# Row-wise infinity norm of an 8192 x 8192 matrix: other runs of rows, another list of tail loads, eight load semaphores for five

## The chip, the core and the metric

One Trainium2 chip, one NeuronCore of it. The engines that matter here are VectorE (DVE in the profile), which reduces; GpSimd (POOL), which combines partial results; SyncE (SP) and ScalarE (ACT), whose queues issue DMAs; and the core's 16 DMA engines, which move data between DRAM and SBUF. SBUF has 128 partitions; a tile is written "partitions x columns". The metric is the device time of one execution in microseconds (us), as a median of several; lower is better.

## The reference

```python
def setup_inputs():
    return {"x": np.random.randn(8192, 8192).astype(np.float32)}

def reference(x):
    return np.linalg.norm(x, ord=np.inf, axis=1)
```

With `axis=1` the infinity norm of a row is the largest absolute value in it. So 268 MB of float32 are read, each element once, and 8192 numbers come out.

## The kernel before

**Which row lies where.** The kernel splits the rows into a main part and a tail of `ROWS` x 128 rows. In both, a partition holds consecutive rows of `x`, which lie in DRAM without a gap: 46 rows a partition in the main part, 18 in the tail. A row is 8192 columns, 32 KiB. Neighbouring partitions therefore read from addresses that lie 46 x 32 KiB and 18 x 32 KiB apart.

**Main part.** 23 loads of two rows a partition (16384 columns, 64 KiB a partition, 8.4 MB in all) go to `ring`, a buffer in SBUF of `RING` = 3 x 16384 columns, so to three places in turn. Each is reduced by one `tensor_reduce` (maximum of absolute values), which writes two numbers a partition to `res_big`.

**Tail.** The 18 rows of a partition are taken as one line of 147,456 columns and cut into loads of falling size. `tail_loads` plans the cuts: from the last load (`FIRST` = 768 columns) backwards, it makes each load as large as the reductions behind it leave time for, by the prices `LOAD` and `REDUCE` (us a column, us fixed). The result is 29 loads, in the order of issue of 16384, 10048, 14528, 8192 (3 times), 8448, 9088, 8064, 7168, 5632, 5696, 5056, 4224, 3968, 3136 (twice), 2752, 2496, 2176, 1920, 1600, 1472, 1344, 1152, 1024, 896, 768 and 704 columns. The load before the last is the end of the last row but one; the last load is the end of the last row.

A load can hold the end of a row, whole rows, and the beginning of another; `parts` lists these pieces, each with its own reduction. Where a row has several pieces, their results go to a small tile `parts<row>`, and GpSimd combines them with `tensor_scalar` (L207), up to two more values in one instruction. The last row differs: the results of its earlier pieces are written in `ring` just behind the place of the last load (`spots`, beyond `RING`), so that the last reduction takes the 704 loaded columns and the 6 results beside them at once, 710 elements.

**Order and waits.** `Pieces.load` issues each load on SP's queue and has it add 16 to one of `SEMS` = 5 semaphores, used in turn. `Pieces.reduce` waits on that semaphore. A load waits for two things: that the reduction of the load five before it is done (one load at a time on a semaphore, L97 to L103), and that the columns of the ring which it overwrites have been reduced (the framework finds that). `Pieces.room` gives places in the ring one after another; where the rest is too short for a load, it starts at 0 again. All loads are in one queue: SP issues them in order, so a load that waits holds up those behind it.

**The end.** ACT stores `res_big` and the first `ROWS` - 2 columns of `res_tail`, both after the reduction of the load two before the last (L221, L225, L229). SP waits for GpSimd's last combination (L236) and for VectorE, stores the last two columns (L240), and waits for ACT's stores and its own.

Of the kernel before, what the change touches and what calls it, by code (L numbers as in the profile page):

```python
# [8 lines left out]
R = 2  # L9
RING = 3 * 16384  # L10
APART = 2048
SEMS = 5


LOAD = (1.1775e-3, 0.073)
REDUCE = (1.0417e-3, 0.060)
SPARE = 0.08
ROWS = 18
FIRST = 768
SNAP = 0.6  # L20
GRAIN = 64

IDLE = 2


def tail_loads(n_cols, big):

    slack = 0.0
    lag = REDUCE[0] * FIRST + REDUCE[1]
    loads = []
    end = ROWS * n_cols

    def take(top, bottom, most):
        nonlocal slack  # L40
        w = 0
        n = 0
        spare = SPARE if loads else 0
        while True:

            n += 1
            start = max(bottom, (top - 1) // n_cols * n_cols - (n - 1) * n_cols)
            fit = int((lag + slack - spare - REDUCE[1] * n) / REDUCE[0])
            w = max(w, min(fit, top - start) // GRAIN * GRAIN)
            if fit <= top - start or start <= bottom:  # L50
                break
        w = max(GRAIN, min(w, most, top - bottom))
        row = (top - w + n_cols - 1) // n_cols * n_cols
        if top - row >= SNAP * w or (w == most and top > row):
            w = top - row
        n = (top - 1) // n_cols - (top - w) // n_cols + 1
        slack += (LOAD[0] - REDUCE[0]) * w + LOAD[1] - REDUCE[1] * n
        loads.append((top - w, w))
        return top - w

    ends = [take(end, end - n_cols, FIRST), take(end - n_cols, end - 2 * n_cols, n_cols)]
    for top, bottom in zip(ends, (end - n_cols, 0)):
        while top > bottom:
            top = take(top, bottom, big)
    return loads[::-1]


class Pieces:
# [7 lines left out]
    def __init__(self, tc, ring):  # L76
        self.tc, self.nc, self.ring, self.head = tc, tc.nc, ring, 0
        self.sems = [tc.alloc_semaphore(f"loaded{i}") for i in range(SEMS)]
        self.started = self.reduced = 0
# [9 lines left out]
    def load(self, at, w, src):  # L89
        i = self.started  # L90
        self.started += 1
        ins = self.nc.sync.dma_start(out=self.ring[:, at : at + w], in_=src)  # L92
        ins.then_inc(self.sems[i % SEMS], 16)
        self.tc.no_tile_sem_insts.add(ins.ins.name)
        self.tc.declare_no_dep(ins.ins, group="loads", reason="a reduction stands in between")
        self.tc.add_to_no_dep_group("loads", ins.ins)
        if i >= SEMS:  # L97
            self.tc.add_manual_dep(
                ins.ins,
                self.last[i - SEMS].name,  # L100
                mybir.DependencyInfo(mybir.DependencyClass.Sync, mybir.DependencyReason.DATA),
# [3 lines left out]
    def reduce(self, pairs):  # L105
# [3 lines left out]
        for k, (dst, src) in enumerate(pairs):  # L109
# [9 lines left out]
            else:  # L119
                ins.wait_op(self.sems[i % SEMS], 16 * (i // SEMS + 1), "sem-ge")  # L120
            self.tc.declare_no_dep(ins.ins, group="loads", reason="waits on the load's semaphore")
# [5 lines left out]
def kernel(  # L127
# [6 lines left out]
    f32 = mybir.dt.float32  # L134
    n_rows, n_cols = x.shape

    tail = tail_loads(n_cols, R * n_cols)
    split = n_rows - ROWS * P
    n_big = split // (R * P)

# [7 lines left out]
    res_big = single.tile([P, n_big, R], f32)  # L148
    res_tail = single.tile([P, ROWS], f32)
    idle = single.tile([1, IDLE], f32)  # L150
    pieces = Pieces(tc, ring)

    for t in range(n_big):
        at = pieces.room(R * n_cols)
# [6 lines left out]
    for i, (start, w) in enumerate(tail):  # L161
        c = 0
        while c < w:
            row = (start + c) // n_cols
            n = min(w - c, (row + 1) * n_cols - start - c)
            parts.append((row, i, c, n))
            c += n
    of_row = [[q for q in parts if q[0] == row] for row in range(ROWS)]

# [3 lines left out]
    at = RING  # L173
    for row, own in enumerate(of_row):
        if row == ROWS - 1:
            spots[own[-1][1]] = at
# [13 lines left out]
    for i, (start, w) in enumerate(tail):  # L190
        at = spots[i] if i in spots else pieces.room(w)
# [7 lines left out]
        )  # L199
        for row in range(ROWS - 1):  # L200
            if len(of_row[row]) > 1 and of_row[row][-1][1] == i:
# [78 lines left out]
```

## Time and profile before

| | us |
|---|---|
| median of 3 runs (628.87 to 628.91) | 628.88 |
| the profiled execution | 628.88 |
| its span on the chip | 627.1 |
| DVE busy | 552.1 (62 instructions) |
| POOL busy | 3.2 (14 instructions) |
| DVE waiting for loads before the 23 big reductions | 69.4 (22.5 of it for the first) |
| DVE waiting for loads in the tail | 2.1 and 1.2 |

The page gives, for each engine, busy time and its share of the span; for 40 equal slices the busy share in tenths; and for each group of instructions the source line, engine, operation, `output<-input` by tile name, shape and count, then busy time, mean ns of one, and the idle time before them with what ended it. `L110` is line 110 of the kernel. A `q` behind an engine's name (`SPq`) means its queue, which issues DMAs. The busy time by stretch has, in this order: the stretch in us from the span's start, its length, DVE's busy time (and instructions), POOL's, the clock granted to the matrix engine (not used here), the DMA engines' busy share and the GB/s that they moved. The order of time has: start, duration, engine, line, operation, tiles, shape and count, and in brackets the idle time before.

The waits on SP's own queue show what holds loads back: 455.9 us for reductions of `res_big`, 82.3 for those that write `parts`, 59.2 for those that write `res_tail`, 3.8 for those that write `ring`; the longest single one is 37.7 us. The loads' time from issue to landing is 21.8 us for the first, about 40.8 for big ones, and 4.1 for the last.

### The profile page before, as it was taken

The numbers are of one execution on the slowest core, as the hardware profiler recorded it, in microseconds if no ns is written. First come the engines' busy times: TensorE is split into PE (matmuls) and PEld (weight loads), VectorE is DVE, ScalarE is ACT, GpSimd is POOL, SyncE is SP. The second block draws the span as 40 slices with busy tenths as digits, with TensorE's granted clock in tenths as the row PEclk, the third lists the DMA queues.
The fourth block names the chain that finished last, engine by engine and source line by source line (L and its number), as shares of the span: only waits on it lengthen the run. The fifth ranks groups of instructions, "written<-read, shape, count | busy, mean of one in ns | idle before, by whom it ended". The sixth has DMA issues, their size and how long they took to land.

```text
span 627.1 us, 175 instructions
## 1 busy us (share of the span) xinstructions
DVE 552.1 (88%) x62; POOL 3.2 (1%) x14
## 2 busy tenths in 40 slices
DVE  0588988889988889888898888988889999999998
POOL 0000000000000000000000000000000000000000
DMA  9999999999999999999999999999999999999997
GB/s 401 410 460 401 468 401 468 401 468 401 468 401 468 401 468 401 468 401 468 401 464 405 451 418 451 418 439 431 422 437 442 404 435 442 430 422 430 426 422 308
DMA packets 7921, 268.48 MB, mean 428 GB/s; under 512 B 1264, under 2 KB 1264, under 8 KB 2416
## 3 DMA queue, kind: packets, MB, share of 16 engines
q1 hardware_dynamic: 7632, 268.44, 99.3%
q10 hardware_dynamic: 288, 0.03, 0.0%
q14 instruction: 1, 0.01, 0.0%
HBM read 268.44 MB, written 0.03 MB: 428 GB/s over the span
## 4 chain that ended last, share of the span: by engine, by line
DMA 57%; DVE 42%; issue 0%; DVEq 0%; SPq 0%
DMA ring<-in_x_dram 57%; DVE res_big L110 22%; DVE parts L110 12%; DVE res_tail L110 7%; DVE ring L110 1%; DVEq L275 0%; SPq L92 0%; DVE idle L218 0%
## 5 line engine op out<-in xcount | busy, mean ns | idle before, releaser
L110 DVE TENSOR_REDUCE res_big<-ring 128x2 f32<-128x16384 f32 x23 | 396.1, 17220 | 69.4 <-DMA ring<-in_x_dram 69.4
L110 DVE TENSOR_REDUCE parts<-ring 128x1 f32<-128x3136 f32 (+18 forms) x22 | 78.5, 3634 | 1.2 <-DMA ring<-in_x_dram 1.2
L110 DVE TENSOR_REDUCE res_tail<-ring 128x1 f32<-128x8192 f32 (+1 forms) x9 | 69.8, 7811 | 2.1 <-DMA ring<-in_x_dram 2.1
L110 DVE TENSOR_REDUCE ring<-ring 128x1 f32<-128x1600 f32 (+5 forms) x6 | 8.3, 1445 | 0.0
L207 POOL TENSOR_SCALAR res_tail<-parts 128x1 f32<-128x1 f32 x9 | 2.7, 296 | 615.6 <-DVE parts L110 615.6
L207 POOL TENSOR_SCALAR parts<-parts 128x1 f32<-128x1 f32 x1 | 0.4, 353 | 5.6 <-DVE parts L110 5.6
L264 POOL MEMSET const-bfloat16-1.0<- 128x1 bf16 x1 | 0.1, 101 | 0.0
L264 POOL MEMSET const-uint8-127<- 128x1 uint8 x1 | 0.1, 101 | 0.0
L264 POOL MEMSET const-float32-0.0<- 128x1 f32 x1 | 0.1, 99 | 0.2 <-issue 0.2
L264 POOL MEMSET const-float32-1.0<- 128x1 f32 x1 | 0.1, 98 | 0.0
L218 DVE MEMSET idle<- 1x1 f32 x2 | 0.1, 59 | 0.0
## 6 DMA issues: line engine op xcount, KB each, us to landing
ring<-in_x_dram SPq DMA_DIRECT2D x3, 4096.0 KB, 40.5
ring<-in_x_dram SPq DMA_DIRECT2D x1, 7264.0 KB, 31.1
ring<-in_x_dram SPq DMA_DIRECT2D x1, 5024.0 KB, 33.3
ring<-in_x_dram SPq DMA_DIRECT2D x1, 4544.0 KB, 34.6
ring<-in_x_dram SPq DMA_DIRECT2D x1, 4224.0 KB, 40.3
ring<-in_x_dram SPq DMA_DIRECT2D x1, 4032.0 KB, 35.5
ring<-in_x_dram SPq DMA_DIRECT2D x1, 3584.0 KB, 35.4
ring<-in_x_dram SPq DMA_DIRECT2D x2, 1568.0 KB, 18.3
```

The lines of the kernel that those rows point to most:

```text
L110: ins = self.nc.vector.tensor_reduce(out=dst, in_=src, axis=mybir.AxisListType.X, op=mybir.AluOpType.max, apply_absolute_value=True,)
L207: combined = nc.gpsimd.tensor_scalar(out=to, in0=best, scalar1=two[0], scalar2=two[1] if len(two) == 2 else None, op0=mybir.AluOpType.max, ...
L218: rest = nc.vector.memset(idle[:, i : i + 1], 0.0)
L264: nc = _bacc.Bacc("TRN2", target_bir_lowering=False, num_devices=1)
```

## The change

The tail has 16 rows a partition instead of 18, so the main part has 48 instead of 46 and 24 big loads instead of 23. `tail_loads` no longer plans: a written list `TAIL` of 28 sizes takes its place, from 13504 columns to two of 640. The function lays them one after another; the load before the last is the last 640 columns of the last row but one, as before in kind, and the last row is begun before it. `SEMS` is 8. Nothing else is changed; the code that makes pieces, places, waits and stores works from these values. By it, VectorE has 66 reductions instead of 60 and GpSimd 14 combinations instead of 10; the last reduction takes 640 loaded columns and 7 results.

```diff
-SEMS = 5
-
-
-LOAD = (1.1775e-3, 0.073)
-REDUCE = (1.0417e-3, 0.060)
-SPARE = 0.08
-ROWS = 18
-FIRST = 768
-SNAP = 0.6
-GRAIN = 64
+SEMS = 8
+
+
+ROWS = 16
+TAIL = [13504, 13632, 12160, 10816, 9664, 8576, 7616, 6784, 6080, 5376, 4800, 4288, 3776, 3392]
+TAIL += [2944, 2624, 2368, 2048, 1792, 1152, 1472, 1280, 1088, 960, 832, 768, 640, 640]
...
-def tail_loads(n_cols, big):
...
+def tail_loads(n_cols):
+    last_row = (ROWS - 1) * n_cols
+    loads = []
+    at = 0
+    for w in TAIL[:-2]:
+        loads.append((at, w))
+        at += w
+        if at + TAIL[-2] == last_row:
+            at = last_row
+    loads += [(last_row - TAIL[-2], TAIL[-2]), (at, TAIL[-1])]
+    assert sum(TAIL) == at + TAIL[-1] == ROWS * n_cols
+    return loads
...
-    tail = tail_loads(n_cols, R * n_cols)
+    tail = tail_loads(n_cols)
```

More of the change, by code (lines that the diff above doesn't have):

```diff
@@ L11 @@
 APART = 2048
-SEMS = 5
-LOAD = (1.1775e-3, 0.073)
-REDUCE = (1.0417e-3, 0.060)
-SPARE = 0.08
-ROWS = 18
-FIRST = 768
-SNAP = 0.6
-GRAIN = 64
+SEMS = 8
+ROWS = 16
+TAIL = [13504, 13632, 12160, 10816, 9664, 8576, 7616, 6784, 6080, 5376, 4800, 4288, 3776, 3392]
+TAIL += [2944, 2624, 2368, 2048, 1792, 1152, 1472, 1280, 1088, 960, 832, 768, 640, 640]
 IDLE = 2
-def tail_loads(n_cols, big):
-    slack = 0.0
-    lag = REDUCE[0] * FIRST + REDUCE[1]
+def tail_loads(n_cols):
+    last_row = (ROWS - 1) * n_cols
     loads = []
[L37 to L65, printed above, removed]
+    at = 0
[7 more added lines that the diff above has]
+    return loads
 class Pieces:
```

## The prediction

> **What bounds the kernel now.** I read the page's head and the row of slices first, then the busy time by stretch, then the instructions in order of time, then the rows by shape. The page says that one thing never stops:
>
> ```profile
> span 627.1 us, 175 instructions
> DVE 552.1 (88%) x62; POOL 3.2 (1%) x14
> DMA  9999999999999999999999999999999999999997
> HBM read 268.44 MB, written 0.03 MB: 428 GB/s over the span
> ```
>
> The DMA engines are full in every slice but the last, VectorE works 88% of the span. The busy times of three stretches (big loads; the first two tail loads; the rest) show what changes on the way:
>
> ```profile
> 22.50:467.60 445.10, 396.05 (x23) 0.00 (x0) 1.00 1.00 433
> 467.60:496.70 29.10, 27.88 (x5) 0.00 (x0) 1.00 0.99 428
> 496.70:624.90 128.20, 128.20 (x35) 3.02 (x10) 1.00 0.99 422
> ```
>
> The reader is to see that DMA keeps its pace (433 GB/s, 422 with small loads), while VectorE, idle 49 us of the first 445, is busy for all of the last 128.2. Both end together, and the order of time shows how closely:
>
> ```profile
> 22.50 17.22 DVE L110 TENSOR_REDUCE res_big<-ring 128x2 f32<-128x16384 f32 x1 [22.50 <-DMA ring<-in_x_dram]
> 41.85 17.22 DVE L110 TENSOR_REDUCE res_big<-ring 128x2 f32<-128x16384 f32 x1 [2.13 <-DMA ring<-in_x_dram]
> ...
> 467.62 25.87 DVE L110 TENSOR_REDUCE res_tail<-ring 128x1 f32<-128x8192 f32 x3 [2.13 <-DMA ring<-in_x_dram]
> 493.41 2.08 DVE L110 TENSOR_REDUCE parts<-ring 128x1 f32<-128x1856 f32 x1
> 496.68 6.75 DVE L110 TENSOR_REDUCE parts<-ring 128x1 f32<-128x6336 f32 x1 [1.20 <-DMA ring<-in_x_dram]
> ...
> 623.27 0.37 ACTq L221 DMA_DIRECT2D out_dram<-res_big  x1
> ...
> 624.01 0.89 DVE L110 TENSOR_REDUCE res_tail<-ring 128x1 f32<-128x710 f32 x1
> ...
> 624.84 0.06 DVE L218 MEMSET idle<- 1x1 f32 x2
> 624.92 0.35 SPq L240 DMA_DIRECT2D out_dram<-res_tail  x1
> ```
>
> Big loads arrive every (467.62 - 22.50)/23 = 19.353 us and are reduced in 17.22. From 496.68 VectorE never waits visibly. The trace's landing records show that the loads do not run far ahead: the last one lands at 623.95, 0.06 before its reduction. So the end is the last landing, plus 0.06, plus one reduction of 0.89, plus what follows it (627.10 - 624.90 = 2.20), plus 628.88 - 627.10 = 1.78 outside the span. The profiled execution took 628.88, the median of the runs.
>
> **Prices.** Loads: from one landing to the next, 16384 columns take 19.354 us and 768 take 0.98, a line of about 0.073 us + 1.1775 ns a column; it meets the 28 landings between to about 0.02 us; the last load, with none behind it, is 0.06 cheaper. Reductions:
>
> ```profile
> L110 DVE TENSOR_REDUCE parts<-ring 128x1 f32<-128x7936 f32 x1 | 8.4, 8409 | 0.0
> L110 DVE TENSOR_REDUCE parts<-ring 128x1 f32<-128x768 f32 x1 | 0.9, 945 | 0.0
> L110 DVE TENSOR_REDUCE res_tail<-ring 128x1 f32<-128x710 f32 x1 | 0.9, 885 | 0.0
> ```
>
> (8409 - 945)/(7936 - 768) = 1.041 ns a column and 0.145 us fixed. Neighbours overlap: three of 8192 fill 467.62 to 493.41, 8.597 each, so one costs 0.06 us + 1.0417 ns a column of VectorE's time, and the last one of a row of them 0.085 more.
>
> **The change part by part.**
>
> *Number and bytes of loads: nothing.* Before, 23 + 29 = 52 loads; after, 24 + 28 = 52, of the same 524,288 columns. At the line above all landings add up to the same, and the last stays at 623.95 if the queue never runs dry and a column costs what it did.
>
> *Does VectorE keep up with the new list?* I walked both lists with these prices (landing after landing; a reduction starts 0.02 after its landing or when the one before lets it). The walk gives the old kernel's last landing as 623.95 and its end as 624.90, as measured. For the new list: the 13504 columns land at 483.6, VectorE comes free from the last big one at 484.9; the 13632 land at 499.72 when it has been idle 0.7; from there 117,568 columns in 40 reductions need 117,568 x 1.0417 ns + 40 x 0.06 + 0.085 = 124.96 us, so they could end at 499.75 + 124.96 = 624.71. The other path is the last landing, 623.95 + 0.03 + the last reduction. So VectorE's six extra instructions (66 reductions for 60, 0.36 us) lie in idle time before 499.75 and in some 0.09 us after. Without that cover they would cost 0.36.
>
> *A shorter last load.* 640 columns and 7 partial results are 647 instead of 710: 63 x 1.0417 ns = 0.066 us less.
>
> *Start after landing.* 0.06 before, 0.03 in the walk. Along the new list the walk's lag is 0.02 to 0.09 (0.58 once, at 1152), so this is between 0.04 gained and 0.03 lost; I take -0.03, the place's own value.
>
> *The ring.* The 10816 columns no longer fit behind 12160 (50,112 of 49,152), go to place 0, and leave 9,856 columns unused, so that load must wait for the 13504 to be reduced, to 499.2. On SP the seven loads behind it wait as well. It is needed once the load before it has landed at 514.1, less 2.4 us of start (21.78 us from the first issue to the first reduction, less 19.35): 511.7, so 12.5 us cover the wait; without them it would cost its lateness one for one.
>
> *Eight semaphores.* They let a load be issued three reductions earlier. The walk finds the closest issue 4.4 us ahead of need (0.8 before, with none late), and with five it ends at the same time: no gain. What seven loads in flight instead of four cost isn't shown: from below nothing (the pace was one line with two, three or four in flight), from above a second 0.073 for each of 28, 2.0 us. I take nothing, the nearer row.
>
> *Stores.* ACT's two wait for the reduction of the load two before the last, now of 768 columns; it ends at 623.33 by the walk, some 0.15 later than before. The first store took until 1.6 us after issue, the second 2.1; so the second is done near 626.0, before SP's last at 624.8 + 1.4 = 626.2. Were they 0.3 later, they would decide. GpSimd makes 14 combinations for 10, the last of 0.36 us from 624.24 to 624.60, 0.19 before VectorE ends.
>
> *Where the rows lie.* A partition's rows in DRAM start 48 x 32 KiB = 1536 KiB apart instead of 1472, and in the tail 512 KiB instead of 576. No row has these distances. From below, nothing: 1472 and 576 agree (the first tail load, 16384 columns, lands 19.36 us after its forerunner; a 64 KiB packet takes 2.42 us in both, 2.415 to 2.434 over all but the first 16). From above: the one place where 16 streams hamper each other is the start, whose first packets take 3.06 us on average, 0.64 more; if every one of the 52 loads began so, 33 us. I take nothing, because the two measured distances are the nearest rows. DMA has no cover: a per cent on all columns is 6.2 us, and VectorE's idle time doesn't help.
>
> The Trainium skill speaks against this part. "DMA: Bandwidth & Descriptors", section "Latency and other measured facts", has copies at a row pitch of 512 KiB at 207 GB/s where a pitch padded by 4 KiB reached 214, and far less from 2 MiB on. No run here shows it, as 1472 and 576 KiB are no such pitches; by that ratio 617 us of loads would grow by an estimated 21 us, to some 649.
>
> The same page's "Rules for kernel authors" wants 1 MiB or more a DMA, and its fit charges about 2 us to each; 640 columns are 320 KiB. This trace charges 0.073 us in a filled queue, so the page's price is hidden here and the sum doesn't take it.
>
> Sum: -0.07 - 0.03 = -0.10 us: 628.78.
>
> **The rivals.**
> 1. *Distance of the rows, big loads (slower).* Sixteen streams whose rows start at multiples of 512 KiB hamper one another. For: nothing ahead of the DMA, every slice full. Against: packets even to 0.02 us at both old distances. Price: the start's 0.64 us again in each of 24 big loads, 15.4 us: 644.2; between 2 and 33 according to how often it strikes. It decides from 0.2% of the loads' time on.
> 2. *Distance of the rows, tail alone (slower).* The same only at 512 KiB: 27 tail loads behind the first, between a tenth and half of 0.64 each, 2 to 9 us; at a quarter 4.3 us: 633.1. VectorE idles instead.
> 3. *Depth of the queue (slower).* Seven loads in flight double each load's fixed part: +2.0, 630.8. For: stretches with small loads are at 422 rather than 433 GB/s. Against: that loss is already the 0.073.
> 4. *Faster.* The new distances would have to load faster than 433 GB/s; 0.2% of 617 us is needed. Nothing in the packets points there.
>
> That the change does nothing but shift pieces is the forecast itself.
>
> **How the numbers follow.** The forecast is 628.78, its own range 628.70 to 628.95 (lag of the start, stores). I give it 0.44; rival 1 0.28, rival 2 0.15, rival 3 0.10, faster 0.03. The unshown price of the distance is what keeps the forecast under a half: DMA alone sets the end and nothing hides it. A difference under 0.2% (1.26 us) is about what a measurement of this kernel can tell from no change. So faster 0.03, within 0.44, slower 0.53. The range begins at 628.6 and goes to 650, which takes in rivals 2 and 3 and most of rival 1, not its far end (33 us, 662).
>
> **What would show it.** Big reductions still 19.35 us apart: the distance costs nothing. If 19.5 or more, rival 1; if only the tail's stretch falls below 422 GB/s and VectorE has idle time in it, rival 2 or 3 (3 if large loads keep the pace). VectorE idle about 0.7 us near 499, none that counts after; the last reduction of 647 columns at 0.82 us. Wrong would be a landing gap from the ring's wait near 514 to 527, or stores that end after SP's last.

## The result and the profile after

The changed kernel takes 629.71 us (median of 22 executions, 629.49 to 630.13) against 628.87 for the kernel before (22 executions, 628.74 to 629.16): +0.84 us, a ratio of 1.0013 with a 95% interval of 1.0008 to 1.0019. That is within the 0.2% taken for no change, but not the 0.10 us less that was forecast: the new kernel is measurably slower.

The head of its page, as it stood for the kernel before:

```profile
span 628.1 us, 186 instructions
DVE 552.6 (88%) x68; POOL 4.5 (1%) x18
DMA  9999999999999999999999999999999999999997
HBM read 268.44 MB, written 0.03 MB: 427 GB/s over the span
```

The span is 1.0 us longer (the profiled execution took 629.86), DVE has six instructions more and only 0.5 us more work, and the DMA engines are as full as before. The busy time of two stretches, big loads and tail (stretch, length, DVE, POOL, clock, DMA share, GB/s), shows where to look:

```profile
23.00:468.10 445.10, 396.05 (x23) 0.00 (x0) 1.00 1.00 433
468.10:625.80 157.70, 156.49 (x45) 4.30 (x14) 1.00 0.99 420
```

For the kernel before, the same cut gives 433 GB/s and, for the tail,

```profile
467.60:624.90 157.30, 156.08 (x39) 3.02 (x10) 1.00 0.99 423
```

So the big loads keep their pace, the tail is 0.4 us longer, and everything in the new kernel is already half a microsecond late when the tail begins. The order of time tells both places:

```profile
22.99 17.22 DVE L78 TENSOR_REDUCE res_big<-ring 128x2 f32<-128x16384 f32 x1 [22.99 <-DMA ring<-in_x_dram]
42.32 17.22 DVE L78 TENSOR_REDUCE res_big<-ring 128x2 f32<-128x16384 f32 x1 [2.11 <-DMA ring<-in_x_dram]
...
468.16 17.22 DVE L78 TENSOR_REDUCE res_big<-ring 128x2 f32<-128x16384 f32 x1 [2.13 <-DMA ring<-in_x_dram]
...
500.23 3.15 DVE L78 TENSOR_REDUCE parts<-ring 128x1 f32<-128x2880 f32 x1 [0.67 <-DMA ring<-in_x_dram]
...
586.04 30.02 DVE L78 TENSOR_REDUCE parts<-ring 128x1 f32<-128x4096 f32 x12 [0.49 <-DMA ring<-in_x_dram]
...
625.02 0.82 DVE L78 TENSOR_REDUCE res_tail<-ring 128x1 f32<-128x647 f32 x1
```

The first load is reduced at 22.99 instead of 22.50: 0.49 us late at the start, 0.54 at 468.16. Then, at 586.04, VectorE waits 0.49 us for the load of 4800 columns. The walk has no wait there. The last reduction starts 1.01 us later than before and takes 0.07 less.

The trace's landing records show what happened to the 4800 columns. Each of the 16 DMA engines reports its part; 15 of them came between 584.78 and 585.46, and the last at 586.02. One packet of 19,200 bytes, begun at 584.17, took 1.376 us where all others of its size took 0.72. That engine stayed 0.6 us behind the others to the end, and every later load landed when it was done.

Just before, at 583.85, an engine carried something that isn't a load. The DMA queues in two windows, after the change from 583 to 585 us:

```profile
q1 hardware_dynamic: 59, 0.81, 96.9%
q14 instruction: 1, 0.01, 1.0%
```

and in the kernel before from 624 to 625 us:

```profile
q10 hardware_dynamic: 288, 0.03, 22.0%
q14 instruction: 1, 0.01, 3.0%
```

`q14` fetches instructions, 8192 bytes in one packet. Each of the two kernels has one such fetch in its span. Before the change it came beside the stores (`q10`), after the last load; now it falls among the loads.

### The profile page after: what moved, and what is told of

Its sections match the earlier page's. It is cut to its first block, busy times and chain, and to the rows that moved or that the text cites. A ratio compares the mean times of both kernels' runs of the same rounds, so it can differ in the third digit from the quotient of the medians.

```text
span 628.1 us, 186 instructions
## 1 busy us (share of the span) xinstructions
DVE 552.6 (88%) x68; POOL 4.5 (1%) x18
## 4 chain that ended last, share of the span: by engine, by line
DMA 64%; DVE 35%; issue 0%; DVEq 0%; SPq 0%
DMA ring<-in_x_dram 64%; DVE res_big L78 22%; DVE parts L78 9%; DVE res_tail L78 3%; DVE ring L78 1%; DVEq L243 0%; SPq L60 0%; DVE idle L186 0%
## 5 line engine op out<-in xcount | busy, mean ns | idle before, releaser
L78 DVE TENSOR_REDUCE res_big<-ring 128x2 f32<-128x16384 f32 x24 | 413.3, 17220 | 72.1 <-DMA ring<-in_x_dram 72.1
L78 DVE TENSOR_REDUCE parts<-ring 128x1 f32<-128x1280 f32 (+28 forms) x31 | 104.8, 3447 | 1.2 <-DMA ring<-in_x_dram 1.2
L78 DVE TENSOR_REDUCE res_tail<-ring 128x1 f32<-128x8192 f32 (+1 forms) x4 | 26.8, 6711 | 0.0
L78 DVE TENSOR_REDUCE ring<-ring 128x1 f32<-128x1152 f32 (+6 forms) x7 | 8.4, 1268 | 0.0
```

Source lines behind the costliest of these rows:

```text
L78: ins = self.nc.vector.tensor_reduce(out=dst, in_=src, axis=mybir.AxisListType.X, op=mybir.AluOpType.max, apply_absolute_value=True,)
```

## The experiments

Three parts of the change were separated first: the runs of rows, the list of loads, the semaphores. All times below are medians of 10 or 11 executions (four for one kernel, named there), beside the kernel before on the same chip (628.83 to 628.88).

**Runs of 48 and 16 rows alone** (kernel before)

```diff
-ROWS = 18
+ROWS = 16
```

> Runs of 48 and 16 rows alone, with the planned list (the same 28 cuts) and five semaphores. If the distance of the rows costs the time: about 0.8 us above the kernel before (some 629.7), with packets over 2.45 us in the big loads as after the change. If the list or the semaphores cost it: as before, 628.9.

629.37 us (629.23 to 629.58), +0.49, ratio 1.0008 [0.9999, 1.0017]; the interval just reaches 1, but no execution of the one lies among those of the other (628.72 to 629.10). Neither theory alone fits: this is a little over half of the loss. In its order of time the loss is there at the first load and stays the same:

```profile
23.12 17.22 DVE L110 TENSOR_REDUCE res_big<-ring 128x2 f32<-128x16384 f32 x1 [23.12 <-DMA ring<-in_x_dram]
42.45 17.22 DVE L110 TENSOR_REDUCE res_big<-ring 128x2 f32<-128x16384 f32 x1 [2.11 <-DMA ring<-in_x_dram]
...
61.80 17.22 DVE L110 TENSOR_REDUCE res_big<-ring 128x2 f32<-128x16384 f32 x1 [2.13 <-DMA ring<-in_x_dram]
```

23.12 - 22.50 = 0.62 us at the start, then steps of 19.33 and 19.35. The tail from 468.2 to 625.3 moves 423 GB/s, as before: 512 KiB between partitions costs nothing there.

**The list and eight semaphores without the runs** (changed kernel)

```diff
-ROWS = 16
-TAIL = [13504, 13632, 12160, 10816, 9664, 8576, 7616, 6784, 6080, 5376, 4800, 4288, 3776, 3392]
+ROWS = 18
+TAIL = [16384, 13504, 13632, 12160, 10816, 9664, 8576, 7616, 6784, 6080, 5376, 4800, 4288, 3776, 3392]
```

> The new list and eight semaphores with runs of 46 and 18 rows (one load of 16384 columns put ahead of the list). If the distance of the rows costs the time: 628.78, 0.1 us under the kernel before, last landing near 623.95. If the list or the depth of the queue costs it: about 629.7, with a single late packet in the tail as after the change.

629.47 us, +0.59, ratio 1.0010 [1.0001, 1.0019]: the other part of the loss, with the late packet of 19,200 bytes at 583.82 (1.376 us again). The addresses of that load differ from those in the changed kernel, the packet is the same.

**The changed kernel with five semaphores, and the kernel before with eight**

```diff
-SEMS = 8
+SEMS = 5
```

> The changed kernel with five semaphores instead of eight. If the depth of the queue (seven loads in flight) costs the time: 628.8. If the distance of the rows does: still about 629.7.

```diff
-SEMS = 5
+SEMS = 8
```

> The kernel before with eight semaphores. If the depth costs the time: about 629.7, if not 628.9; the walk of the prediction says 628.88, no change.

629.74 and 628.88 us, the same as with the other number in each case. The number of semaphores does nothing; rival 3 falls.

That left the fetch as the suspect for the list's part, and the question which engine's program sets it off. VectorE has six instructions more, GpSimd four.

**Eight tiny memsets ahead, on VectorE or on GpSimd**

```diff
     pieces = Pieces(tc, ring)
+    early_pad = single.tile([1, 8], f32)
+    for i in range(8):
+        nc.vector.memset(early_pad[:, i : i + 1], 0.0)
```

(`nc.gpsimd` in the other pair; once in the kernel before, once in the new list with runs of 46 and 18 rows.)

> The kernel before with 8 tiny memsets on VectorE while it waits for the first load; nothing else. Theory: the single 8 KB instruction fetch, seen at 624.4 us in the kernel before and at 583.9 after the change, holds up one DMA engine by 0.66 us, and it is set off by how far VectorE has come in its program. Then it comes earlier by several reductions here, into the loads, and the time rises by about 0.5 us (629.3 to 629.5). Rival: it follows GpSimd's program; then it stays at 624.4 and the time at 628.9.

> The kernel before with 8 tiny memsets on GpSimd at the start. If the fetch follows GpSimd's program it moves ahead of the last load, near 584 or earlier, and the time rises by about 0.5 us. If it follows VectorE's, it stays at 624.4 and the time at 628.9.

> New list with runs of 46 and 18 rows and 8 memsets ahead on VectorE. If the fetch follows VectorE's program: it leaves 583.5 us and comes some eight reductions earlier, with a packet of one DMA engine held up at its new place; the time stays near 629.5. If it follows GpSimd's: it stays at 583.5.

> New list with runs of 46 and 18 rows and 8 memsets ahead on GpSimd. If the fetch follows GpSimd's program: it moves to about the start, or eight combinations earlier (before 503 us), and the late packet of 19200 bytes is gone. If VectorE's: it stays at 583.5 and the time at 629.5.

Measured: 629.56, 628.80, 629.46 and 629.49 us. Eight instructions that are done before there is any data make the kernel before 0.69 us slower (ratio 1.0012 [1.0002, 1.0021]) if they are VectorE's, and not if they are GpSimd's. The DMA queues of the first from 559 to 561 us:

```profile
q1 hardware_dynamic: 31, 0.89, 105.5%
q14 instruction: 1, 0.01, 1.0%
```

The fetch has gone from 624.5 to 559.7, and a packet there took 0.658 us more than others of its size. On the list it moved from 583.5 to 542.5 with VectorE's memsets and stayed at 583.4 with GpSimd's. From the packet records of all these kernels:

```
kernel            DVE instr.  fetch at   packet held up     took, usual (us)   time, us
before              62        624.45     none                                   628.87
rows18_plan8        62        624.37     none                                   628.88
before_pool8        62        624.49     none                                   628.80
rows16_plan5        61        625.02     none                                   629.37
after               68        583.85     19200 B at 584.17   1.376, 0.719       629.71
rows18_list8        69        583.49     19200 B at 583.82   1.376, 0.719       629.47
list_pool8          69        583.38     19200 B at 583.70   1.376, 0.718       629.49
before_dve8         70        559.68     28672 B at 560.00   1.725, 1.067       629.56
list_dve8           77        542.53     34304 B at 542.85   1.932, 1.274       629.46
```

The packet held up takes 0.657 or 0.658 us longer each time, whatever its size. That is not all that its engine loses. The records do not name the engine, but the times pair: each fetch among the loads begins as a load packet ends on one engine, and that engine's next packet, the one held up, begins 0.31 to 0.32 us late, when the fetch is done. So in the five kernels of the table with a packet held up, its engine loses 0.97 to 0.98 us. A load is done when the slowest of the 16 engines is, so the kernel pays that loss less the engine's lead over the slowest: after the change the struck engine was 0.41 us ahead, and then 0.56 behind the next one.

**The list with VectorE's program made short again**

```diff
+    more = sorted((q for q in parts if q[2] > 0 and q[0] < ROWS - 2), key=lambda q: q[3])
+    parts = [q for q in parts if q not in more[:7]]
     of_row = [[q for q in parts if q[0] == row] for row in range(ROWS)]
```

> The new list with runs of 46 and 18 rows and eight semaphores, but seven small pieces of rows 5, 8, 9, 11, 12, 14 and 15 of the tail (10,304 of 147,456 columns) are not reduced, so that VectorE's program is as long as in the kernel before (60 reductions instead of 67). Loads are the same. If the instruction fetch costs the time: the fetch is back at about 624 us, no packet is late in the tail, the last load lands near 623.95 and the time is 628.8. If the list of loads itself costs it: the packet of 19200 bytes is late as before and the time 629.4.

628.74 us (628.64 to 628.92), 0.09 less than the kernel before in the same runs, ratio 0.9999 [0.9989, 1.0008]. All loads of the new list are there, and eight semaphores. Its DMA queues from 624 to 625 us have the fetch behind the loads:

```profile
q10 hardware_dynamic: 279, 0.03, 21.4%
q14 instruction: 1, 0.01, 2.8%
```

No packet of the tail is late. So the loads of the list cost nothing by themselves, and its 0.6 us are the fetch. This is the other direction of the test above. But the kernel leaves out the reductions of seven pieces, 10.7 us of VectorE's time (552.7 us busy in `rows18_list8`, 542.0 here), and VectorE then waits for loads where the full list may not. Its last eight reductions start 0.02 to 0.10 us after their landings, as in the walk (0.02 to 0.09). Whether VectorE keeps up with all pieces of the list when no fetch falls among the loads is not shown.

**Another list, at a length in between** (changed kernel)

```diff
-SEMS = 8
...
-ROWS = 16
-TAIL = [13504, 13632, 12160, 10816, 9664, 8576, 7616, 6784, 6080, 5376, 4800, 4288, 3776, 3392]
-TAIL += [2944, 2624, 2368, 2048, 1792, 1152, 1472, 1280, 1088, 960, 832, 768, 640, 640]
+SEMS = 5
...
+ROWS = 18
+TAIL = [16384, 14400, 13056, 11584, 10112, 9920, 8000, 8000, 6848, 5824, 5376, 4928, 4416, 4032]
+TAIL += [3456, 3136, 2432, 2432, 2176, 1984, 1728, 1472, 1280, 1152, 896, 896, 768, 768]
```

> Another list of 28 tail loads for runs of 46 and 18 rows, with 40 reductions in the tail, three instructions of VectorE more than in the kernel before and four fewer than the new list at these runs; five semaphores. The walk ends 0.05 us earlier than before. If the fetch stays behind the loads at this length of program: 628.8. If it falls among them: about 629.4 with one late packet. Either way it narrows at which length the fetch moves.

629.49 us, with the fetch at 587.6 and a packet that takes 0.658 us longer. DVE has 65 instructions here. So the fetch stays behind the loads up to 62 and falls among them from 65 on; at which of them it changes was not tried.

**The fetch during the first load** (kernel before with 64 memsets on VectorE, in the same way)

> The kernel before with 64 tiny memsets ahead on VectorE, done before the first load lands. By the theory the instruction fetch comes some 5 us after the start, during the first load. If an engine's delay is never made up: 629.3 to 629.5 as with 8 memsets. If it is lost in the scatter of the engines' starts: 628.9.

629.43 us, +0.60. The fetch came at 7.34 us and the packet at 7.65 took 2.949 us for 2.42; the first reduction starts at 23.17 instead of 22.50, and in the landing records one engine stays 0.55 to 0.61 us behind the others to the end. None of the places among the loads where the fetch fell (7, 543, 560, 583 to 584 and 588 us) was free.

**Rows 2 MiB apart** (kernel before, partition rows taken from one block of 64)

```diff
-    x_big = x[:split].rearrange("(p t r) m -> t p (r m)", p=P, r=R)
-    x_tail = x[split:].rearrange("(p r) m -> p (r m)", p=P)
+    x_all = x.rearrange("(p r) m -> p (r m)", p=P)
+    n_main = n_rows // P - ROWS
+    x_tail = x_all[:, n_main * n_cols :]
...
-        pieces.load(at, R * n_cols, x_big[t])
+        pieces.load(at, R * n_cols, x_all[:, t * R * n_cols : (t + 1) * R * n_cols])
```

(The stores of `out` follow the same rows.)

> The kernel before, but a partition takes 64 consecutive rows: the first 46 are the main part, the last 18 the tail, so that neighbouring partitions lie 2 MiB apart in all loads. If distances that are multiples of 512 KiB slow every load: 16384 columns take well over 19.35 us and the time is some tens of per cent longer (the page's ratio of 164 to 214 would make an estimated 800 us). If they disturb only the start: 629.3 to 630. If they do nothing: 628.9.

656.96 us (four executions, 655.45 to 658.61), ratio 1.0439 [1.0417, 1.0462]. That is none of the three expected outcomes. The busy time of four stretches has DMA's rate in the last column:

```profile
26.50:131.80 105.30, 86.56 (x6) 0.00 (x0) 1.00 0.99 401
131.80:480.00 348.20, 309.53 (x19) 0.00 (x0) 1.00 1.00 433
480.00:606.90 126.90, 125.69 (x22) 1.67 (x6) 1.00 1.00 428
606.90:654.90 48.00, 31.50 (x18) 1.35 (x4) 1.00 0.90 242
```

The distance of the rows does matter: the first reduction starts at 26.57 and the first six loads are slow. Then the loads run at the old 433 GB/s for 348 us, at the same distance, and only the small loads at the end fall back: 242 GB/s, where the kernel before has 390 from 597 us to its end. In the fast stretch the first and the last engine land 3.5 to 3.6 us apart. That the loads are fast because the engines are out of step is argued, not shown; it cannot be all, because in the slow stretch at the end the engines are 3.6 to 8.0 us apart.

A complete kernel that beats both wasn't found. The list may be worth some 0.1 us, less than these runs can tell, and it showed that only with seven of its VectorE instructions left out; giving small pieces to GpSimd was not tried.

## Why the prediction was wrong

*"So VectorE's six extra instructions (66 reductions for 60, 0.36 us) lie in idle time."* This is the step that failed. The six were costed by what they take to run, and that part held: VectorE idles 0.67 us at 500.23 (0.7 predicted). Their other cost was not looked for: a longer program is fetched at another time, over the same DMA engines, which have no idle time. It measured +0.59 us with the list at the old runs of rows, and +0.69 with nothing but eight idle instructions.

The view that would have warned was on the page: one packet in an instruction queue, in the kernel before at 624.45 us, half a microsecond after the last landing of 623.95. Its place was luck that the sum took for granted.

*"Where the rows lie ... I take nothing."* Wrong in size: the term is 0.49 us in the median, where the sum had 0 and the upper bound 33. Rival 1 was right that the distance costs time in the big loads, but it is paid once, in the first load, and not per load. So the sign that was to clear the distance, big reductions 19.35 us apart, was met (19.33 to 19.49, most 19.35) while it cost 0.49. The row that the price was taken from does not explain it either: the first 16 packets take 3.03 to 3.10 us on average in the three kernels with 48 rows, and 3.01 to 3.17 in those with 46. What differs is the rest of that load: 5, 6 and 32 of its other 112 packets took over 2.45 us, and with 46 rows none or one. Why only there isn't shown. In the three kernels with 48 rows the first reduction starts at 22.99 to 23.17; with 46 rows and no fetch in that stretch, in nine kernels, at 22.43 to 22.78. Rival 2, the tail alone, did not happen (423 GB/s in the tail with 16 rows and 18 alike).

In the medians the two losses do not add: 0.49 + 0.59 would be 1.08, both together cost 0.84, more than the larger alone. In the profiled execution of the changed kernel they do: 0.49 us late at the start, 0.56 for the engine held up and 0.07 less for the last reduction make 0.98, and it was 0.98 us longer than the profiled one before (629.86 and 628.88). What a fetch costs depends on the struck engine's lead over the slowest; in the records of the eight kernels with a fetch among the loads that engine is then 0.51 to 0.82 us behind the next one. That this is why the medians show less was not tested.

*The pieces that held.* Number and bytes of the loads: the same pace, a line of 0.073 us + 1.1775 ns a column, met again. The walk of the new list: 628.78 predicted, 628.74 with the fetch out of the way, but with seven reductions left out and at the old runs of rows, so this agreement is in part luck. The shorter last reduction: 0.82 us for 647 values. Its start after the landing, predicted 0.03, was 0.03 without the fetch and 0.06 after the change. The ring's wait for the 10816 columns: issued at 499.6 (499.2 predicted), no gap behind it. Eight semaphores: nothing, in both directions. The stores: after the list without the fetch, SP's last still ends the kernel.

The Trainium skill, "DMA: Bandwidth & Descriptors", section "Latency and other measured facts", was cited against the change; it has copies at 207 and 164 GB/s for 512 KiB and 2 MiB, where 214 was full. The size doesn't hold here: the tail at 512 KiB kept 423 GB/s as at 576, and at 2 MiB the big loads had 433 once past the first six; the total at 2 MiB was 4.4% longer, not the 30% of an estimate by that page's ratio; but the small loads at 2 MiB lost more than that ratio (242 for 390 GB/s). The measurement decides. The fit of 2 us a DMA that the prediction set aside stands on that page for DMAs issued from GpSimd; the loads here come from SP.

The same page, section "Queues, rings and completion order", has each DMA engine serve its queues in turn and lists refill among the uses of queue row 14, which agrees with the `q14` packet between two load packets of one engine. "Runtime: NRT & Kernel Launch", section "Instruction fetch mechanics", calls such a refill mostly hidden. For VectorE it is: no instruction waited for it. For a kernel whose DMA engines are full it isn't: 0.6 us.

## What to carry to other kernels

Where DMA alone sets the end, count every packet that its engines carry, the instruction fetches too: look up in the profile when they come, and see that none falls among the loads, because what one engine loses there is not made up while the queue stays full (0.55 to 0.61 us behind from the first load to the last, with the fetch at 7 us). An instruction can cost more by its place in the program than by its run time; adding idle ones to one engine is a cheap test that tells the two apart. And when an edit changes two things that both touch the slowest of many parallel engines, don't count on their prices to add.

## What the hardware showed that was not expected

- An 8192-byte instruction fetch among the loads, itself 0.31 to 0.33 us long, lets the next load packet of its engine begin 0.31 to 0.32 us late and makes it 0.657 us longer, whether that packet has 17,664, 19,200, 28,672 or 34,304 bytes (0.53 us at 65,536). Why it is this much was not found out.
- When it comes follows VectorE's instructions, not GpSimd's: with 61 or 62 of them it comes beside the last reduction, with 65 to 77 after 44 to 46 have started. With 126, 64 of them memsets at the start, it came at 7.34 us, after the 64 and before the first reduction, so a count of 45 is no general rule. Numbers in between were not tried.
- The start of the loads depends on where 128 rows lie. At 46 rows apart the first reduction starts at 22.4 to 22.8 us, at 48 at 23.0 to 23.2, at 64 (2 MiB) at 26.6, while big loads then run at 433 GB/s for all three (at 64 only after the first six).
